# Weight-quarter sums of a hybrid layer's feed-forwards: from vector additions to accumulating DMAs in DRAM, with seven and five tiles done by quarters instead of six and four

## The chip, the cores and the metric

The kernel runs on one core of one Trainium2 chip. The metric is device time in microseconds (us) of one execution; the median over several runs is compared. The core has TensorE (PE, the matrix unit, with PEld for its weight loads), VectorE (DVE), ScalarE (ACT) and GpSimd (POOL), which compute, and SyncE (SP), which in this kernel does nothing but issue DMAs. Each engine works through its own queue of instructions in order and waits on semaphores for the others. A DMA is issued by an engine's queue and then runs beside the engines. SBUF is the on-chip memory with 128 partitions, PSUM holds the results of TensorE (eight banks of 128x512 fp32), and DRAM is the memory outside.

## The reference

One layer, batch 1, 512 tokens (T), width 1024 (D), fp32:

```python
x = x + 0.5 * rms_norm(swiglu_ffn(rms_norm(x, g0), ffn1_w_in, ffn1_w_out), p0)
x = x +       rms_norm(token_mixer(rms_norm(x, g1), ...), p1)
x = x + 0.5 * rms_norm(swiglu_ffn(rms_norm(x, g2), ffn2_w_in, ffn2_w_out), p2)

def swiglu_ffn(x, w_in, w_out):            # w_in 1024 x 5632, w_out 2816 x 1024
    gate, up = jnp.split(x @ w_in, 2, axis=-1)
    return (jax.nn.silu(gate) * up) @ w_out
```

`token_mixer` projects to 3592 columns, runs two causal mixers (HGRN2 with four heads, mLSTM with four heads) over the tokens, and projects back through a 1024 x 1024 matrix. The change touches only the second product of each feed-forward, `h @ w_out` with `h` 512 x 2816, and the places from which some of its preparation is issued.

## The kernel before

**Precision.** Every fp32 operand is split into a high part (rounded to fp32r by a cast) and a low part (the rest), and a product is three matmuls: high by high, high by low, low by high. A weight tile is 256 x 512 or 1024 x 128, 512 KB, 128 partitions by 1024 values. It is loaded by SP (`load`, L236) into a buffer of one of two rings, `raw` (three buffers) or `raw2` (five). ACT casts it into one of four weight slots (L273, the high part), and DVE subtracts to get the low part (L275). `split` holds these steps. `feed` calls it until four slots are taken, `pull` gives the next prepared tile to TensorE, `drop` frees its slot.

**Order.** The program is one Python generator run from top to bottom. `weights` walks a list of `Item`s, one for each tile that TensorE uses; an `Item` has a key and the `Load`s that belong to it. From the ring's depth and the `ahead` of a `Load`, `weights` works out after which item a load may be issued, and `load_due` issues it at the end of that item's `split`. `behind(...)` makes what is issued inside it follow the given instructions in the order of the scheduler, which otherwise places instructions of each engine by their dependencies. Most SP waits are for a ring's buffer to be read by ACT and DVE.

**Feed-forward, first product.** `ffn_in` runs through `ORDER` (or `ORDER2` in the second feed-forward), a list of pairs (product, tile). There are eleven tiles of 256 hidden rows. Each is made with seven products instead of eight, of halves of the inner dimension, of the columns and of the tokens (`prod`, matmuls at L603, 24 for each product). Sums of weights that these need are made by DVE in the raw buffers (L289). At the end all hidden values lie in `hf`.

**Feed-forward, second product.** `ffn_out` makes two halves of 512 output columns, one after the other. For each half it goes through the eleven tiles in the order `OUT[half]`. For every (half, tile) a weight tile of 256 hidden rows by 512 columns is used. It is done in one of two ways.

- *Plainly* (`plain`, L893): four blocks of 128 tokens, two of 256 columns, two of 128 hidden rows, three matmuls: 48 matmuls of 256 columns each.
- *By quarters* (`quartered` and `product`, L901), for the tiles in `QUARTERED[half]`. The weight tile is four quarters of 128 hidden rows by 256 columns, and the hidden tile is four quarters as well. Seven products of six matmuls, 42 in all, take sums of quarters on both sides (the Strassen-Winograd scheme). Four of the products go to banks shared by all such tiles of the half (`M`), three straight into the output's banks `C`. After the half's last tile by quarters `common` (L925) combines the four shared banks into `T`, and `add` (L863 in the half's last matmuls) adds these into the output.

Such a tile pulls two weight tiles: first the quarters as loaded, less quarter 0 which no product needs (so the split has 768 columns), then their four sums. `sum_quarters` (L306) makes these on DVE, four additions of 128x256 in place in the raw buffer, as the last thing that the first split does; the second `Item` has no load and reads the same buffer.

On the hidden side `h_quarters` splits the left quarters (ACT L812, DVE L813), either into places in buffers that held the input (`PLACES`, tiles 2, 4, 6, 8) or into two buffers of the ring `raw`. `h_sums` makes the sums of the hidden quarters (DVE L844, four additions), `s_tile` splits these. `more(n)` keeps such work two to three tiles ahead of TensorE. What is made for a tile stays for the second half if that half also does it by quarters. A plain tile's hidden part is `h_tile`; `LATER` gives buffers to some of them, and those in `AGAIN` are kept from the first half.

The last four tiles of the second half (`LAST`) are done otherwise: all four weight tiles are held, one in each slot, and TensorE goes through them token block by token block, so that the norm behind the product (`last`, `post1`) can begin with the first tokens.

**Mixers.** Between the feed-forwards `mixer` runs the projection's products as jobs: `job_f` (columns as partitions, for forget gates, queries and convolution inputs), `job_t` (tokens as partitions: `hi`, `mv`, `hg`, `mo`). Each `pull`s weight tiles as it goes. Between the jobs' matmuls stand the recurrences, where POOL makes masks: selector masks (L1201) in the HGRN2 part, and the causal mask of the mLSTM scores (L1480), which stands between ACT's exponent (L1479) and DVE's product with the scores (L1490). Before the change POOL's queue issues no DMA there.

## Time and profile before

| | us |
|---|---|
| median of three runs | 936.34 |
| lowest, highest | 936.26, 937.92 |
| the profiled execution, its own time | 936.35 |
| the span of that execution in the profile | 934.6 |

The page of the profile gives the span from the first to the last instruction of the profiled execution, so that about 1.75 us of that execution's time lie outside. The stages in the trace, by the rows in which their instructions run: the first feed-forward's first product up to 224 us, its second product from there to 341.8, the mixers and their output projection to about 560, the second feed-forward's first product to 810.8, and its second product with the norm and the stores to the end.

In the rows of the groups, a line gives the source line, the engine, the operation, the tile written and the tile read with partitions x elements, the count, the busy time and the mean of one in ns, and behind the last bar the idle time of the engine just before these instructions with what ended it. In the rows of a stretch of time the columns are: from and to, length, then busy time and count of PE, PEld, DVE, ACT and POOL, the granted clock of TensorE, the busy share of the DMA engines, and GB/s. In the rows of the timeline they are: start, length, engine, line, operation, tile written and tile read, form, and how many like instructions were joined; idle time before it stands in brackets. A DMA's row in the issues gives the tile, the queue, the count, the size and the median time from issue to landing.

### The profile page before, as it was taken

Reading aid. Unit: us, or ns where it says so; the run is one execution under the profiler, and the core shown is the slowest. Engines: PE = TensorE matmul, PEld = TensorE weight load, DVE = VectorE, ACT = ScalarE, POOL = GpSimd, SP = SyncE. Lnnn points to the kernel's source line nnn. Section 1 sums busy time; section 2 is a strip of 40 time slices with the busy share of each in tenths; the row PEclk is TensorE's granted clock in tenths of the full one; section 3 lists DMA queues with packets and bytes.
Section 4 is the critical chain, followed back from the end, with each engine's and each line's share of the span. In section 5 each row is a group of like instructions: output and inputs, shape, how many; then the busy total and the mean of one; then the engine's idle time right before and its main releaser. Section 6 shows DMA issues by size and latency. Waiting matters only on the chain.

```text
span 934.6 us, 18052 instructions
## 1 busy us (share of the span) xinstructions
PE 926.2 (99%) x7471; PEld 891.8 (95%) x7471; DVE 772.1 (83%) x1044; ACT 511.4 (55%) x735; POOL 106.5 (11%) x172
## 2 busy tenths in 40 slices
PE   9999999999999999999999999999999999999997
PEld 7999999999999999998887887899999999999997
DVE  6899988889988877698766565799899889998884
ACT  7645454557456466956533445595454545655541
POOL 3530000000001045200010310313000000000101
PEclk9999999999999999999999999999999999999999
DMA  9253343332352025421212124352354435334212
GB/s 313 94 157 91 119 132 113 93 112 71 114 177 91 24 72 134 114 70 54 81 46 69 46 91 150 98 181 70 112 158 136 136 116 159 111 91 126 79 46 91
DMA packets 86956, 101.35 MB, mean 108 GB/s; under 512 B 4277, under 2 KB 66777, under 8 KB 86874
## 3 DMA queue, kind: packets, MB, share of 16 engines
q1 hardware_dynamic: 86586, 99.68, 34.9%
q8 instruction: 58, 0.95, 0.4%
q10 hardware_dynamic: 288, 0.52, 0.2%
q14 instruction: 24, 0.20, 0.1%
HBM read 98.10 MB, written 2.10 MB: 107 GB/s over the span
## 4 chain that ended last, share of the span: by engine, by line
PE 62%; ACT 1%; issue 0%; DVE 0%; POOL 0%; DVEq 0%; POOLq 0%; ACTq 0%
PE ps L603 22%; PE ps L893 7%; PE ps L533 6%; PE ps L901 5%; PE ps L179 5%; PE ps L181 5%; PE ps L180 5%; PE ps L1307 2%; PE ps L348 1%; PE ps L543 1%; PE ps L1488 0%; PE ps L1399 0%; PE ps L1600 0%; PE ps L1573 0%; PE ps L1353 0%; PE ps L1597 0%
## 5 line engine op out<-in xcount | busy, mean ns | idle before, releaser
L273 ACT CAST w<-raw 128x1024 fp32r<-128x1024 f32 (+1 forms) x238 | 244.4, 1035 | 231.7 <-PE ps L603 92.8
L275 DVE TENSOR_TENSOR w<-raw,w 128x1024 fp32r<-128x1024 f32 (+1 forms) x238 | 290.9, 1229 | 38.0 <-ACT w L273 37.5
L603 PE MATMUL ps<-xq,w 128*128 128x256 f32 x2016 | 237.1, 277 | 0.0
L603 PEld LDWEIGHTS ps<-xq,w 128*128 128x128 f32 x2016 | 232.9, 188 | 0.0
L603 PE MATMUL ps<-sq,w 128*128 128x256 f32 x1512 | 178.0, 276 | 0.3
L603 PEld LDWEIGHTS ps<-sq,w 128*128 128x128 f32 x1512 | 174.3, 188 | 1.1 <-ACT ps L654 0.9
L893 PE MATMUL ps<-w,hs 128*128 128x256 f32 x960 | 113.0, 276 | 0.0
L893 PEld LDWEIGHTS ps<-w,hs 128*128 128x128 f32 x960 | 110.7, 188 | 0.0
L289 DVE TENSOR_TENSOR raw<-raw,raw 128x1024 f32<-128x1024 f32 x72 | 89.8, 1251 | 8.3 <-DMA raw<-in_ffn_w_in_dram 6.7
L179 PE MATMUL ps<-w,xq 128*128 128x512 f32 x192 | 78.0, 407 | 0.1
L180 PE MATMUL ps<-w,xq 128*128 128x512 f32 x192 | 74.9, 391 | 0.0
L181 PE MATMUL ps<-w,xq 128*128 128x512 f32 x192 | 74.9, 392 | 0.0
L438 POOL TENSOR_SCALAR col<-col 128x1 f32<-128x1 f32 x24 | 8.3, 347 | 513.4 <-ACT junk L437 513.3
L901 PE MATMUL ps<-w,hs 128*128 128x256 f32 x480 | 57.7, 276 | 0.0
L901 PEld LDWEIGHTS ps<-w,hs 128*128 128x128 f32 x480 | 55.9, 188 | 0.0
L533 PE MATMUL ps<-xq,w 128*128 128x256 f32 x480 | 55.7, 278 | 0.0
L533 PEld LDWEIGHTS ps<-xq,w 128*128 128x128 f32 x480 | 54.9, 188 | 0.5 <-issue 0.5
L179 PEld LDWEIGHTS ps<-w,xq 128*128 128x128 f32 x192 | 36.1, 188 | 8.5 <-issue 0.9
L181 PEld LDWEIGHTS ps<-w,xq 128*128 128x128 f32 x192 | 36.0, 188 | 8.0 <-DVE xq L355 0.3
L812 ACT CAST hs<-hf 128x1024 fp32r<-128x1024 f32 x32 | 33.7, 1052 | 17.5 <-PE ps L901 10.8
L180 PEld LDWEIGHTS ps<-w,xq 128*128 128x128 f32 x192 | 36.1, 188 | 7.3 <-DVE w L281 0.3
L813 DVE TENSOR_TENSOR hs<-hf,hs 128x1024 fp32r<-128x1024 f32 x32 | 39.0, 1217 | 1.3 <-ACT hs L812 1.2
(259 smaller groups left out, 1136.8 us busy)
## 6 DMA issues: line engine op xcount, KB each, us to landing
raw<-in_ffn_w_in_dram SPq DMA_DIRECT2D x98, 512.0 KB, 3.7
raw<-in_ffn_w_out_dram SPq DMA_DIRECT2D x44, 512.0 KB, 4.3
raw<-in_w_mix_in_dram SPq DMA_DIRECT2D x28, 512.0 KB, 3.7
raw<-in_w_mix_out_dram SPq DMA_DIRECT2D x8, 512.0 KB, 3.9
out_dram<-xs SPq DMA_DIRECT2D x8, 256.0 KB, 2.0
xs<-in_x_dram SPq DMA_DIRECT2D x6, 256.0 KB, 4.5
gpost<-in_norm_post_dram SPq DMA_DIRECT2D x3, 512.0 KB, 3.6
gpre<-in_norm_pre_dram SPq DMA_DIRECT2D x2, 512.0 KB, 4.8
```

The lines of the kernel that those rows point to most:

```text
L179: mm(ps, sh, mh, start=start, stop=False, **kw)
L180: mm(ps, sh, ml, start=False, stop=False, **kw)
L181: mm(ps, sl, mh, start=False, stop=stop, **kw)
L273: nc.scalar.copy(hi, raw)
L275: self.low = nc.vector.tensor_tensor(lo, raw, hi.bitcast(F32), op=ALU.subtract)
L289: (nc.vector if late else nc.gpsimd).tensor_tensor(o, o, c, op=ALU.add)
L533: mm(ps[:, u0:u1], w[:, a, k, :], self.xop(k, b, u0, u1), start=k + n + m == 0, stop=k == ND - 1 and n == 2, skip_group_check=True,)
L603: self.nc.tensor.matmul(ps[:, c], wb[b][:, k, v], left[d][:, k, :], start=first and a + n + k == 0, stop=n == 2 and k == KH - 1, skip_grou ...
L812: self.nc.scalar.copy(hi, src)
L813: self.nc.vector.tensor_tensor(lo, src, hi.bitcast(F32), op=ALU.subtract)
L893: mm(out, a[kk][:, i * P : (i + 1) * P], w[:, b, kk, QUARTER * v : QUARTER * (v + 1)], start=begin and c == kk == n == 0, stop=kk == 1 and ...
L901: mm(ps[:, QUARTER * c : QUARTER * (c + 1)], A[a][:, c], B[b], start=begin and c == n == 0, stop=n == 2, skip_group_check=True,)
```

## The change

Four things change together.

1. The sums of weight quarters are no longer made by DVE in the raw buffer. A tile in DRAM is kept for each (feed-forward, half, tile by quarters), 24 of them, each four quarters of 128x256. `sums_ahead` fills one. Three copies on SP's queue bring quarter 1, quarter 2 and quarters 2 and 3 of the weights from DRAM to DRAM. Then three DMAs on POOL's queue add: first quarter 0 to the first two, then the first of these to the quarter behind it, then that quarter to the last. Each needs the one before it. The result is in the order (0, 1, 2, 3) of a list that `quartered` reads with `at = (1, 0, 2, 3)`.
2. The second `Item` of a tile by quarters now has a `Load` of its own, of the 512 KB of sums from DRAM into ring `raw2`, where it had none.
3. `sums_due` says for which feed-forward and halves sums are to be made, and each call of `make_sums` starts one tile and moves those under way one step further. The first feed-forward's are made during its `ffn_in`, every fifth product after the fourteenth, and at every other tile of the first half of its `ffn_out`. The second's first half is made in the mixers, at each job of the convolution and each weight tile of `hi` and `mv`; its second half in its own `ffn_in`, every tenth product, and in the first half of its `ffn_out`.
4. Seven tiles are done by quarters in the first half (5 is new) and five in the second (3 is new), in each feed-forward. The order of the second half changes. The left quarters of tiles 5 and 7, which have no place of their own, take one buffer of ring `raw` and the buffer `gpre`, where they took two of `raw`. Tile 0's hidden part loses its place among `LATER`. The last two additions of `h_sums` become one of twice the width.

The diff:

```diff
@@ -79,12 +79,13 @@
-QUARTERED = [(2, 3, 4, 6, 7, 8), (2, 4, 6, 8)]
-OUT = [list(range(PAIRS)), [9, 2, 4, 10, 6, 8, 0, 1, 3, 5, 7]]
-LAST = 4
-PLACES, LATER = {2: 1, 4: 2, 6: 0, 8: 3}, {0: (1, 0), 7: (2, 3)}
+QUARTERED = [(2, 3, 4, 5, 6, 7, 8), (2, 3, 4, 6, 8)]
+OUT = [list(range(PAIRS)), [9, 2, 4, 3, 6, 8, 10, 0, 1, 7, 5]]
+LAST, APART = 4, (5, 7)
+PLACES, LATER = {2: 1, 4: 2, 6: 0, 8: 3}, {7: (2, 3)}
 AGAIN, ROWS = (9, 10), (18, 19, 20, 21)
+EVERY = 5, 10
@@ -136,6 +137,11 @@
         x0 = self.xt[0].rearrange("p (b x) -> p b x", b=2)[:, :, :D].rearrange("p b (k t) -> p b k t", k=KH)
         self.xh = [x0, *self.xq[1:]]
         self.prm = self.cp.tile([P, 36], F32, name="prm")
+        dram = ctx.enter_context(tc.tile_pool(name="sums", bufs=1, space=bass.MemoryType.DRAM))
+        self.sums_of = {
+            (f, h, k2): dram.tile([P, 4, QUARTER], F32, name=f"{f}sums{h}_{k2}")
+            for f in ("f1", "f2") for h in range(2) for k2 in OUT[h] if k2 in QUARTERED[h]
+        }
     def nm(self, s):
         self.uid += 1
@@ -287,8 +293,6 @@
                 late = out[1] >= (HEAD if out[0] == "f1" else 1)
                 (nc.vector if late else nc.gpsimd).tensor_tensor(o, o, c, op=ALU.add)
-        if it.sums:
-            self.sum_quarters(self.quarters(self.raw[it.key]))
         self.load_due(self.done)
         self.done += 1
         yield
@@ -299,11 +303,6 @@
     def quarters(self, v):
         v = self.flat(v)
         return [v[:, QUARTER * j : QUARTER * (j + 1)] for j in range(4)]
-
-    def sum_quarters(self, b):
-
-        for out, a, c in ((1, 1, 0), (0, 0, 2), (2, 1, 2), (3, 2, 3)):
-            self.nc.vector.tensor_tensor(b[out], b[a], b[c], op=ALU.add)
     def both(self, w):
@@ -782,7 +781,10 @@
     def ffn_in(self):
-        for p, t in ORDER2[len(HEADS2) :] if self.second else ORDER[len(HEADS) :]:
+        self.sums_due("f2" if self.second else "f1", (1,) if self.second else (0, 1))
+        for n, (p, t) in enumerate(ORDER2[len(HEADS2) :] if self.second else ORDER[len(HEADS) :]):
+            if n > 14 and n % EVERY[self.second] == 0:
+                self.make_sums()
             with self.behind(*(self.c22 if p == "p3" and self.second else ())):
                 self.feed()
             self.c22 = []
@@ -822,9 +824,12 @@
     def h_quarters(self, k2, n=None):
         src = self.by_chunk(k2)
-        parts = self.x_place(n) if n is not None else [
-            self.wp.tile([P, D], F32R, tag="raw", bufs=RAW, name=self.nm("once"))[:, P - 2 * STEP :] for _ in range(2)
-        ]
+        once = lambda pool, tag, bufs, o: pool.tile([P, D], F32R, tag=tag, bufs=bufs, name=self.nm("once"))[:, o:]
+        if n is not None:
+            parts = self.x_place(n)
+        else:
+            places = [(self.wp, "raw", RAW, P - 2 * STEP), (self.cp, "gpre", 1, STEP // 2)]
+            parts = [once(*places[k2 in APART and m]) for m in range(2)]
         parts = [v[:, : 3 * QUARTER].rearrange("p (k c t) -> p k c t", c=2, t=P) for v in parts]
         self.two_parts(*(v[:, 0] for v in parts), src[:, 0, 1])
         self.two_parts(*(v[:, 1:] for v in parts), src[:, 1])
@@ -844,8 +849,7 @@
         tt = lambda out, x, y, op: self.nc.vector.tensor_tensor(out, x, y, op=op)
         tt(v[:, 0, 0], a[:, 0, 1], a[:, 0, 0], ALU.subtract)
         tt(v[:, 1, 0], v[:, 0, 0], a[:, 1, 0], ALU.add)
-        for k in range(2):
-            tt(v[:, k, 1], a[:, k, 1], v[:, 1, 0], ALU.subtract)
+        tt(v[:, :, 1], a[:, :, 1], v[:, 1:2, 0].broadcast_to([P, 2, 2, P]), ALU.subtract)
         return f
     def s_tile(self, f):
@@ -854,6 +858,29 @@
         self.two_parts(*parts, f)
         parts = [t.rearrange("p k (c u t) -> p k u c t", u=2, t=P) for t in parts]
         return [[t[:, j // 2, j % 2] for j in range(4)] for t in parts]
+
+    def sums_ahead(self, f, h, k2):
+
+        nc, to = self.nc, self.sums_of[f, h, k2]
+        w = (self.ffn1_w_out, self.ffn2_w_out)[f == "f2"][0]
+        q = w[k2 * 2 * P : (k2 + 1) * 2 * P, h * 512 : (h + 1) * 512].rearrange("(k p) (c f) -> p k c f", p=P, f=QUARTER)
+        with self.behind(self.loaded):
+            nc.sync.dma_start(to[:, 0], q[:, 0, 1])
+            nc.sync.dma_start(to[:, 1], q[:, 1, 0])
+            nc.sync.dma_start(to[:, 2:], q[:, 1])
+        yield
+        for a, b, v in ((0, 2, q[:, 0, :1].broadcast_to([P, 2, QUARTER])), (2, 3, to[:, :1]), (3, 4, to[:, 2:3])):
+            nc.gpsimd.dma_start(to[:, a:b], v, accum_op=ALU.add)
+            yield
+
+    def sums_due(self, f, halves):
+        self.ahead, self.making = deque(k for k in self.sums_of if k[0] == f and k[1] in halves), []
+
+    def make_sums(self):
+
+        if self.ahead:
+            self.making.append(self.sums_ahead(*self.ahead.popleft()))
+        self.making = [g for g in self.making if next(g, self) is not self]
     def ffn_out(self, gpost_row, scale, after, trans, head):
@@ -912,11 +939,11 @@
             product(C[1][1], A(3), quarter(w, 3), False)
             product(C[1][0], S(3), quarter(w, 2), False)
             self.drop(w)
-            v = self.pull()
-            product(M["p7"], S(0), quarter(v, 0), begin)
-            product(M["p5"], S(1), quarter(v, 1), begin)
-            product(M["p6"], S(2), quarter(v, 2), begin)
-            product(C[0][1], A(2), quarter(v, 3), False)
+            v, at = self.pull(), (1, 0, 2, 3)
+            product(M["p7"], S(0), quarter(v, at[0]), begin)
+            product(M["p5"], S(1), quarter(v, at[1]), begin)
+            product(M["p6"], S(2), quarter(v, at[2]), begin)
+            product(C[0][1], A(2), quarter(v, at[3]), False)
             self.drop(v)
         def common(M, t):
@@ -965,6 +992,8 @@
                             add(C, T, i % 2)
                     self.drop(w)
                 n += 1
+                if half == 0 and n % 2:
+                    self.make_sums()
                 if n == 1:
                     self.prod("p4", PAIRS - 1)
                     self.after("p4", PAIRS - 1)
@@ -1017,6 +1046,8 @@
     def job_f(self, name, then):
         w, ps = self.pull(), self.ps()
+        if name[0] == "c":
+            self.make_sums()
         for k in range(ND):
             self.in_k(ps, w, k, [(0, HALF), (HALF, T)])
             if k < ND - 1:
@@ -1035,6 +1066,8 @@
         acc = [self.ps() for _ in range(NT)]
         for k2 in range(ND // 2):
             w = self.pull()
+            if name in ("hi", "mv"):
+                self.make_sums()
             for i in range(NT):
                 for kk in range(2):
                     self.t_mm(acc[i], w, 2 * k2 + kk, kk, i)
@@ -1124,9 +1157,11 @@
             for k2 in OUT[h]:
                 src = w_out[k2 * 2 * P : (k2 + 1) * 2 * P, h * 512 : (h + 1) * 512].rearrange("(k p) d -> p k d", p=P)
                 key = (name, "out", h, k2)
-                made.append(Item(key, [Load(key, src, 2, 512, "raw2", 5, 8)], sums=k2 in QUARTERED[h]))
-                if k2 in QUARTERED[h]:
-                    made.append(Item(key, ()))
+                four = k2 in QUARTERED[h]
+                made.append(Item(key, [Load(key, src, 2, 512, "raw2", 5, 8)], sums=four))
+                if four:
+                    key, src = (*key, "sums"), self.sums_of[name, h, k2].rearrange("p (a j) f -> p a (j f)", a=2)
+                    made.append(Item(key, [Load(key, src, 2, 512, "raw2", 5, 8)]))
                 if h == k2 == 0:
                     made.append(Item((name, PAIRS - 1, "a"), ()))
         return made
@@ -1636,6 +1671,7 @@
     def mixer(self):
         nc, tc = self.nc, self.tc
         self.got, self.jobs = set(), deque()
+        self.sums_due("f2", (0,))
         with tc.tile_pool(name="ma", bufs=1) as ma:
             self.vh = ma.tile([P, NT, NH, P], F32, name="vh")
             self.vm = ma.tile([P, NT, NH, 129], F32, name="vm")
```

## The prediction

> **What bounds the kernel now.** I read the page first: busy time, slices, the chain that ended last.
>
> ```profile
> span 934.6 us, 18052 instructions
> PE 926.2 (99%) x7471; PEld 891.8 (95%) x7471; DVE 772.1 (83%) x1044; ACT 511.4 (55%) x735; POOL 106.5 (11%) x172
> PE   9999999999999999999999999999999999999997
> PEclk9999999999999999999999999999999999999999
> PE 62%; ACT 1%; issue 0%; DVE 0%; POOL 0%; DVEq 0%; POOLq 0%; ACTq 0%
> ```
>
> TensorE is busy in 99% of the span and in every slice but the last, at the full granted clock, and no other engine has a visible share of the chain. A busy PE row alone doesn't say that its matmuls follow at their pace, so the next view is the busy time by stretch: start and end, length, then PE, weight loads, DVE, ACT, POOL, clock, DMA share and GB/s.
>
> ```profile
> 56.00:112.00 56.00, 56.00 (x495) 56.00 (x494) 55.59 (x65) 27.80 (x33) 1.30 (x1) 1.00 0.47 142
> 224.00:341.76 117.76, 117.68 (x1038) 117.48 (x1037) 101.28 (x153) 62.87 (x101) 10.17 (x27) 1.00 0.28 86
> 810.80:934.60 123.80, 117.78 (x1040) 117.59 (x1038) 99.89 (x149) 57.93 (x88) 7.05 (x20) 0.99 0.28 90
> ```
>
> The second and third are the two output projections, the only stages where the arithmetic changes. PE has no gap there except after the last matmul; DVE is busy for 101.28 of 117.76 us. The price of one matmul comes from the timeline of PE (start, length, row, count):
>
> ```profile
> 239.00 2.88 PE L901 MATMUL ps<-w,hs 128*128 128x256 f32 x24
> 241.72 0.84 PE L901 MATMUL ps<-w,xq 128*128 128x256 f32 x6
> 312.44 5.60 PE L893 MATMUL ps<-w,xq 128*128 128x256 f32 x48
> 317.88 4.24 PE L893 MATMUL ps<-w,hs 128*128 128x256 f32 x36
> ```
>
> 24 quarter products take 241.72 - 239.00 = 2.72 us, 48 plain ones 317.88 - 312.44 = 5.44 us: 0.1133 us each, either way. (The mean of one in the groups is latency; the matmuls overlap.) A tile done plainly is 48 matmuls, 5.44 us; by quarters 7 products of 6, 42 matmuls, 4.76 us.
>
> **The change, part by part.** *Tiles.* Each feed-forward goes from six and four tiles by quarters to seven and five, so 2 x 2 x 6 = 24 matmuls go: 24 x 0.1133 = 2.72 us. They lie on PE, which sets the end. No PE instruction is added.
>
> *The quarter sums leave DVE, and the four new tiles cost splits.* Rows of the groups (count, busy, mean ns), then single ones:
>
> ```profile
> L306 DVE TENSOR_TENSOR raw<-raw 128x256 f32<-128x256 f32 x80 | 33.7, 421 | 1.6
> L844 DVE TENSOR_TENSOR hf<-hf 128x256 f32<-128x256 f32 x32 | 13.3, 419 | 0.5
> L813 DVE TENSOR_TENSOR hs<-hf,hs 128x1024 fp32r<-128x1024 f32 x32 | 39.0, 1217 | 1.3 <-ACT hs L812 1.2
> L813 DVE TENSOR_TENSOR once<-hf,once 128x256 fp32r<-128x256 f32 (+1 forms) x8 | 4.4, 549 | 0.0
> L812 ACT CAST once<-hf 128x256 fp32r<-128x256 f32 (+1 forms) x8 | 3.8, 511 | 1.8 <-DVE w L275 1.8
> L812 ACT CAST hs<-hf 128x1024 fp32r<-128x1024 f32 x32 | 33.7, 1052 | 17.5 <-PE ps L901 10.8 <-DVE hf L844 4.4 <-PE ps L893 2.3
> 225.24 0.95 DVE L275 TENSOR_TENSOR w<-raw,w 128x768 fp32r<-128x768 f32 x1
> 223.61 0.84 ACT L273 CAST w<-raw 128x768 fp32r<-128x768 f32 x1
> ```
>
> DVE loses 80 sums, 33.7 us. It gains four splits of 768 columns (4 x 0.95), four pieces of left quarters for tile 5 (4 x 0.55), and the sums of hidden tiles, four instructions for each of 12, become three for each of 14, the third twice as wide; priced as two it makes 14 x 4 x 0.42 - 12 x 4 x 0.42 = 3.4. Net 33.7 - 3.8 - 2.2 - 3.4 = 24 us less. ACT gains 4 x 0.84 + 4 x 0.51 = 5.4 us. Neither moves the end: DVE and ACT are hidden by PE in both stages already, so I take 0 for what they gain as well. Through the run of seven quarter tiles DVE needs, per tile, splits of 0.95 and 1.2, 1.22 for the sums of the hidden tile and at most 2.8 for tiles met first: 6.2 us against 4.76 of PE. Before it was 1.7 more (4 x 0.421) and PE had no gap, because much of this is done ahead, in the input projection; the cover grows.
>
> *Two places get tighter.* Tiles 5 and 7 share one buffer for their left quarters, so 7's are made only when PE has finished 5. PE then has tile 6, 4.76 us; the work is the sums of tile 8 on ACT and DVE (1.05 + 1.22) and two pieces of left quarters on DVE (2 x 0.55), 3.4 us. It fits by 1.4. The second is the end of the second half, seen before as:
>
> ```profile
> 318.08 1.05 ACT L273 CAST w<-raw 128x1024 fp32r<-128x1024 f32 x1 [4.06 <-PE ps L893]
> 318.33 1.28 DVE L863 TENSOR_TENSOR ps<-ps,hf 128x512 f32<-128x512 f32 x2
> 319.52 1.21 DVE L275 TENSOR_TENSOR w<-raw,w 128x1024 fp32r<-128x1024 f32 x1
> 321.96 1.52 PE L893 MATMUL ps<-w,xq 128*128 128x256 f32 x12
> ```
>
> The last weight tile is split by 320.73 and used at 321.96: 1.23 us to spare. Now tile 10 holds a buffer until then, so tile 5's hidden part is made in the same place, one more 1.05 on ACT and 1.22 on DVE ahead of that split. Nothing is left to spare; a few tenths are lost, or up to 1.2 us if ACT is late too, in each feed-forward. I take 0.1 each, 0.2 together (0 and 2.4 as ends).
>
> *The DMAs.* Per tile three copies on SP's queue (128, 128, 256 KB, DRAM to DRAM), three accumulations on POOL's queue (256, 128, 128 KB), and a 512 KB load of the sums; 24 tiles: 72 + 72 + 24. No row shows a DRAM-to-DRAM or an accumulating transfer, so bounds (us to landing; then what SP waited for):
>
> ```profile
> q1 hardware_dynamic: 86586, 99.68, 34.9%
> raw<-in_ffn_w_out_dram SPq DMA_DIRECT2D x44, 512.0 KB, 4.3
> gpre<-in_norm_pre_dram SPq DMA_DIRECT2D x2, 512.0 KB, 4.8
> out_dram<-xs SPq DMA_DIRECT2D x8, 256.0 KB, 2.0
> SPq L236 <- DVE w L275: 630.2, 130, 36.8
> ```
>
> A landing takes 2.0 to 4.8 us for plain ones; an accumulation reads its target besides, so twice the upper end, 9.6, is my top. I take 4. Bytes: 99.7 MB took 34.9%; 3 x 12.6 MB more give about 48%, and twice for accumulations 53%: no stretch fills. SP waited 630 us for buffers, so its 96 more issues find room. Loads: two per quarter tile in a ring of five, so 2.5 tiles or 11.9 us ahead, against 4.3 to land. A load of sums now waits on SP for its third accumulation, and the next weight loads stand behind it; in the first half of each feed-forward that accumulation was issued long before. Two loads of mixer weights and the next norm's gain wait on SP for PE to release left quarters (tile 7, then tile 3): at most the rest of a tile, 4.76 us, inside the 11.9. All of this I cost at 0, hidden by PE; if that cover is gone, the split behind a late load is late, and PE after four weight tiles.
>
> *POOL's queue.* An accumulation waits there for the one before it on the same tile, and everything behind it waits too. Behind the sums of the feed-forwards' second halves stand only statistics of the first half, on which the next step of POOL works 37 us later (the last row below, idle time in brackets). In the mixers it matters: seven tiles' sums stand between the selector masks and the causal masks of the mLSTM heads.
>
> ```profile
> 379.68 3.29 POOL L1201 CAST selr<-sel 4x768 fp32r<-4x768 f32 x2
> 391.57 0.37 SPq L236 DMA_DIRECT2D raw<-in_w_mix_in_dram  x1
> 427.81 0.39 PE L179 MATMUL ps<-w,xq 128*128 128x512 f32 x1
> 428.03 0.39 PE L180 MATMUL ps<-w,xq 128*128 128x512 f32 x1
> 441.51 0.37 SPq L236 DMA_DIRECT2D raw<-in_w_mix_in_dram  x1
> 480.45 1.39 POOL L1513 MEMSET C<- 128x1548 f32 x1 [97.48 <-DVE sT L1312]
> 488.14 0.83 POOL L1480 TENSOR_SCALAR_AFFINE_SELECT e<-e 128x512 f32<-128x512 f32 x1 [6.30 <-ACT e L1479]
> 488.38 1.67 DVE L275 TENSOR_TENSOR w<-raw,w 128x1024 fp32r<-128x1024 f32 x1
> 489.97 0.68 DVE L1490 SCALAR_TENSOR_TENSOR pT<-ps,e 128x512 f32<-128x512 f32 x1
> 912.99 0.27 POOL L438 TENSOR_SCALAR col<-col,col 128x1 f32<-128x1 f32 x1 [36.80 <-ACT junk L437]
> ```
>
> The first copies follow the load at 391.57, the last that at 441.51; the first causal mask runs at 488.14 and DVE needs it at 489.97. POOL is empty between 383 and 480. In the order of its queue two tiles are interleaved twice, so the seven wait for 12 landings and 9 issues (0.37 each, as SP's): with 4 us that is 51 us of work, paced by the copies: the last land by 446.3 and are done by 455, 33 us early. Cost 0. DVE's 1.67 instead of 1.21 beside a POOL instruction shows that the two can hold each other up; 0.46 x 72 = 33 us, spread where DVE has just been given 24, moves nothing on PE.
>
> For an accumulation's landing only a page has a price: the Trainium skill, DMA: Bandwidth & Descriptors, section "Anatomy of one DMA — SWDGE (gpsimd) path", gives 2.0 us plus bytes over 436 GB/s; an estimate from it is 2.6 us for 256 KB, and the sum would be the same. A rule speaks against the change: the Trainium skill, SBUF — State Buffer, section "SBUF: two separate sides", says that a DMA issued from POOL can't get its descriptors written while DVE runs an operation that takes the port pair which both share. An estimate by the page's example (3.1 instead of 0.62 us) makes each landing 2.5 us longer, 5.1 us: still nothing on PE, but most of the way to the first rival. No run here shows it yet.
>
> *Sum.* The profiled execution took 936.35 us, span 934.6, and the median is 936.34: 936.35 - 2.72 + 0.2 = 933.8.
>
> **The rivals.** *POOL's queue takes over (slower).* From 396.4 (first copies landed) to 488.14 are 91.7 us; 12 landings and 3.3 us of issues fit up to 7.4 us each. At 9.6 they end at 515, 27 us late; DVE stands at the row of 489.97, weight splits behind it, and PE runs on four weight tiles of 24 x 0.22 = 5.3 us at most. Some 6 to 27 us are lost, I take 12: 946. For it: nothing shows such a transfer. Against: 7.4 is above every landing seen. Chance 0.18.
>
> *The gain is eaten (no change).* The end of the second half loses 1.2 us in each feed-forward, or sums land late once: 936.35 - 2.72 + 2.4 = 936.0. For it: no slack is left there. Against: DVE arrives at both stages with less behind it. Chance 0.18.
>
> *Another gain (it is not only the matmuls).* DVE was the hidden pace and its relief shortens the stages: 1038 matmuls in 117.68 us are 0.1134 each, so at most a few tenths a stage, 932.8 in all. Chance 0.04.
>
> **How the numbers follow.** My forecast, 933.8, has 0.60, between 933.3 and 934.4. What a measurement can tell from no change is about 0.2%, 1.9 us: under 934.5 counts as faster, over 938.2 as slower. The forecast and the third rival are faster, less 0.02 of the forecast that lies over the line; the second rival and most of that are the same; the first is slower, with 0.01 for what I don't see: 0.62, 0.19, 0.19. The range leaves out most of the first rival and reaches over the second: 932.8 to 938.5.
>
> **What would show it.** After: 24 matmuls fewer, pitch still 0.1133, the output stages 1.4 us shorter each; L306 gone and DVE some 24 us lower; POOL's causal mask within a microsecond of ACT's exponent; PE without a wait for a sums load. Wrong would be: landings over 7 us, DVE waiting at the score product for POOL, or PE waiting in the last four tiles of the second half.

## The result, and the profile after

The changed kernel takes 938.1 us in the median of 22 runs (935.98 to 940.84), the kernel before 936.94 us beside it: a ratio of 1.0015, 95% interval 1.0009 to 1.0021. By that ratio it is slower by 1.4 us, less than the 0.2% that the prediction called no change; 933.8 us and a gain of 2.7 us were forecast. A second set of 11 runs (`change_again`) gave 937.76 against 937.0, 1.0011 (0.9999 to 1.0022).

The page of the profile after: span, busy time, two of the queues, and landings (count, KB, median us).

```profile
span 936.2 us, 18261 instructions
PE 924.4 (99%) x7447; PEld 889.9 (95%) x7447; DVE 751.0 (80%) x966; ACT 516.7 (55%) x743; POOL 174.8 (19%) x244
q1 hardware_dynamic: 100410, 124.85, 43.0%
q0 software_dynamic: 13440, 12.59, 10.2%
raw<-in_ffn_w_in_dram SPq DMA_DIRECT2D x98, 512.0 KB, 4.8
f1sums<-in_ffn_w_out_dram POOLq DMA_DIRECT2D x12, 256.0 KB, 7.6
f2sums<-in_ffn_w_out_dram SPq DMA_DIRECT2D x24, 128.0 KB, 3.8
f2sums<-in_ffn_w_out_dram SPq DMA_DIRECT2D x12, 256.0 KB, 6.7
f2sums<-in_ffn_w_out_dram POOLq DMA_DIRECT2D x12, 256.0 KB, 6.9
f2sums<-f2sums POOLq DMA_DIRECT2D x24, 128.0 KB, 3.5
```

24 matmuls are gone, and DVE has 21 us less. But PE, which waited nowhere in the second feed-forward's input projection, now waits there once. L621 (L622 before) holds DVE's operations on finished products in PSUM; here it is a subtraction for which PE's next product waits. First that wait of PE after, then DVE's timeline up to it, after and (last fence) before:

```profile
PE ps L602 <- DVE ps L621: 2.1, 1, 2.1
```

```profile
761.37 1.22 DVE L295 TENSOR_TENSOR raw<-raw,raw 128x1024 f32<-128x1024 f32 x1 [4.27 <-DMA raw<-in_ffn_w_in_dram]
762.52 0.69 DVE L621 TENSOR_TENSOR ps<-ps,hf 128x512 f32<-128x512 f32 x1
...
772.38 0.69 DVE L621 TENSOR_TENSOR ps<-ps,hf 128x512 f32<-128x512 f32 x1
773.22 1.05 PE L602 MATMUL ps<-sq,w 128*128 128x256 f32 x7 [2.15 <-DVE ps L621]
```

```profile
759.65 1.23 DVE L289 TENSOR_TENSOR raw<-raw,raw 128x1024 f32<-128x1024 f32 x1 [2.54 <-DMA raw<-in_ffn_w_in_dram]
760.79 0.69 DVE L622 TENSOR_TENSOR ps<-ps,hf 128x512 f32<-128x512 f32 x1
...
770.66 0.69 DVE L622 TENSOR_TENSOR ps<-ps,hf 128x512 f32<-128x512 f32 x1
```

A weight load lands 1.72 us later (761.37 against 759.65). From there DVE works without a pause to the subtraction that PE needs, in both kernels, so all of it arrives at PE; PE itself is 0.37 us ahead there, and so it waits 2.1. The load in question was issued at the same time in both kernels, after and then before:

```profile
754.26 0.37 SPq L242 DMA_DIRECT2D raw<-in_ffn_w_in_dram  x1
```

```profile
754.27 0.94 SPq L236 DMA_DIRECT2D raw<-in_ffn_w_in_dram  x1
```

These two traces have no landing for it. `copies_at_the_place` and `sums_alone`, below, have: there the load issued at this place lands at 761.22 and 761.25, and DVE's addition starts 0.12 later. So the load takes longer. What changed is the traffic. From 752 to 762 us, after and then before (DMA share and GB/s at the end):

```profile
752.00:762.00 10.00, 9.91 (x87) 9.71 (x87) 5.73 (x6) 3.04 (x4) 1.17 (x1) 1.00 0.95 249
```

```profile
752.00:762.00 10.00, 9.91 (x88) 9.71 (x87) 7.46 (x8) 3.89 (x6) 0.00 (x0) 1.00 0.62 197
```

The copies for the third tile of the second half were issued at 749.95 to 751.14, the first accumulation at 754.64.

The end is late too. The program's closing line, after and then before (ns min/median/max, first and last start):

```profile
L1861 POOLq DRAIN  x3: 38/102/5013, 930.4 to 935.9; - x3
L1861 SPq DRAIN  x3: 7/7/7, 934.5 to 935.6; - x3
```

```profile
L1825 POOLq DRAIN  x3: 39/78/656, 929.7 to 934.4; - x3
L1825 SPq DRAIN  x3: 7/7/7, 933.9 to 934.2; - x3
```

POOL's closing drain takes 5.01 instead of 0.66 us. It starts at 930.36 behind POOL's last instruction and ends at 935.37, 0.8 us after SP is done with the stores. Before, it was over 3.5 us ahead of SP.

The start of each matmul after, less its start before, tells where the time went (us, along the time of before; worked out from both traces, for this kernel and those of the experiments):

| | 36 | 220 | 338 | 670 | 768 | 790 | last matmul |
|---|---|---|---|---|---|---|---|
| the change | 0.09 | 0.09 | -1.27 | -1.18 | -0.37 | 1.73 | 0.37 |
| change_again | 0.25 | 0.25 | -1.11 | -0.99 | -1.01 | 1.05 | -0.31 |
| tiles_alone | 1.18 | 1.18 | 1.94 | 1.97 | 2.03 | 2.43 | 2.97 |
| copies_alone | 0.67 | 0.66 | -0.70 | -0.68 | -0.65 | 1.04 | -0.32 |
| copies_at_the_place | 0.70 | 0.70 | 0.70 | 0.79 | 0.79 | 1.71 | 1.71 |
| sums_earlier | 0.58 | 0.58 | -0.78 | -0.65 | 8.82 | 8.52 | 7.16 |
| second_in_first | 0.50 | 0.50 | 8.04 | 8.30 | 8.52 | 8.70 | 7.34 |
| first_alone | -0.15 | -0.15 | -1.51 | -1.52 | -1.52 | -0.92 | -0.92 |
| all_but_last_again | 0.79 | 0.79 | -0.57 | -0.43 | -0.24 | 0.27 | -0.11 |

Each output projection gives its 1.36 us, twice (0.09 to -1.27, and 1.73 to 0.37). The sum of the profile: -2.72, start 0.09, drift 0.09, slower pace of the matmuls from 677 to 697 us 0.81, the wait 2.10, ACT's last statistic 0.28 later behind PE, drain and closing 0.87: 1.52, and the spans differ by 1.53. The first column is chance: before, profiled again, is itself 0.72 late there. So is part of the pace: the change's second profile has no slower stretch at 677, but the wait of 2.1 and the drain again.

### The profile page after: what moved, and what is told of

It is laid out like the page before. It is cut to its first block, busy times and chain, and to the rows that moved or that the text cites. A ratio compares the mean times of both kernels' runs of the same rounds, so it can differ in the third digit from the quotient of the medians.

```text
span 936.2 us, 18261 instructions
## 1 busy us (share of the span) xinstructions
PE 924.4 (99%) x7447; PEld 889.9 (95%) x7447; DVE 751.0 (80%) x966; ACT 516.7 (55%) x743; POOL 174.8 (19%) x244
## 4 chain that ended last, share of the span: by engine, by line
PE 62%; ACT 1%; DVE 0%; issue 0%; POOL 0%; DVEq 0%; POOLq 0%; ACTq 0%
PE ps L602 22%; PE ps L928 6%; PE ps L532 6%; PE ps L920 6%; PE ps L185 5%; PE ps L187 5%; PE ps L186 5%; PE ps L1342 2%; PE ps L347 1%; PE ps L542 1%; PE ps L1523 0%; PE ps L1434 0%; PE ps L1635 0%; PE ps L1608 0%; PE ps L1388 0%; PE ps L1632 0%
## 5 line engine op out<-in xcount | busy, mean ns | idle before, releaser
L279 ACT CAST w<-raw 128x1024 fp32r<-128x1024 f32 (+1 forms) x242 | 248.1, 1031 | 206.3 <-PE ps L602 91.2
L281 DVE TENSOR_TENSOR w<-raw,w 128x1024 fp32r<-128x1024 f32 (+1 forms) x242 | 295.7, 1225 | 36.7 <-ACT w L279 35.6
L814 ACT CAST hs<-hf 128x1024 fp32r<-128x1024 f32 x34 | 35.8, 1053 | 37.0 <-PE ps L928 22.0
L815 DVE TENSOR_TENSOR hs<-hf,hs 128x1024 fp32r<-128x1024 f32 x34 | 41.5, 1222 | 18.2 <-ACT hs L814 18.1
L873 POOL DMA_DIRECT2D f2sums<-in_ffn_w_out_dram x12 | 15.9, 1322 | 133.2 <-DMA f2sums<-in_ffn_w_out_dram 133.0
```

Source lines behind the costliest of these rows:

```text
L279: nc.scalar.copy(hi, raw)
L281: self.low = nc.vector.tensor_tensor(lo, raw, hi.bitcast(F32), op=ALU.subtract)
L814: self.nc.scalar.copy(hi, src)
L815: self.nc.vector.tensor_tensor(lo, src, hi.bitcast(F32), op=ALU.subtract)
```

## The experiments

**The two parts apart.** The tiles, the order and the places of the change, with `sum_quarters` kept on DVE and no DMAs:

```diff
-QUARTERED = [(2, 3, 4, 6, 7, 8), (2, 4, 6, 8)]
+QUARTERED = [(2, 3, 4, 5, 6, 7, 8), (2, 3, 4, 6, 8)]
...
```

> Seven and five tiles by quarters, in the new order and with the new places, but the sums of weight quarters made by DVE in the raw buffers as before: no DMA in DRAM, none on POOL's queue. Theory A (the tiles give the 2.72 us that the matmuls are worth, and the DMAs take it back by late weight loads and by POOL's closing drain): 936.9 - 2.7 = 934.2 us, PE 2.7 us less busy and no wait on PE over 0.5 us. Theory B (DVE, or the new order, eats the gain): 936 to 938 us, with a wait of PE on a split or on a hidden tile in an output projection.

940.2 us, 1.0032 (1.0020 to 1.0043). Theory B, and more than it foresaw: with the sums still on DVE the tiles cost time. Instead of gaining 1.36 us the two output projections lose 0.76 and 0.54 (table). PE's waits there that are long enough to be listed (in all, times, longest), then the busy times in the run of seven tiles, here and (last fence) in the change:

```profile
PE ps L903 <- DVE w L275: 1.9, 4, 0.7
```

```profile
249.00:274.00 25.00, 24.12 (x207) 23.72 (x206) 24.48 (x35) 16.12 (x19) 0.00 (x0) 1.00 0.36 115
```

```profile
249.00:274.00 25.00, 25.00 (x223) 25.00 (x223) 19.89 (x22) 15.60 (x18) 2.84 (x3) 1.00 0.94 276
```

DVE is full, 24.48 of 25 us, and PE has 16 matmuls fewer in it. In the change DVE has 5 us to spare there. So the gain is had only if sums leave DVE in the run of seven tiles. Those of the second half matter less: `first_halves`, below, leaves them on DVE and loses 0.3 us for it.

The other part alone, the sums in DRAM with the old tiles and order:

```diff
-QUARTERED = [(2, 3, 4, 5, 6, 7, 8), (2, 3, 4, 6, 8)]
+QUARTERED = [(2, 3, 4, 6, 7, 8), (2, 4, 6, 8)]
...
```

> Six and four tiles by quarters in the old order, but the sums made in DRAM by the DMAs (60 accumulations instead of 72). Theory A: 936.9 + 2.1 (PE waiting for DVE's L621 in the second feed-forward's input projection) + 0.9 (POOL's closing drain, 5.0 instead of 0.7 us) = 939.9 us. Theory B: 936.9 us.

938.88 us, 1.0020 (1.0011 to 1.0028). PE waits 0.9 us for L621 at the same place, less than half of what was expected; the drain takes 4.03 us and is hidden. The median is 2.1 us up; 0.9 of it is this wait, and the rest is not explained.

**Where the second half's sums are made.** In the mixers (`sums_due("f2", (0, 1))`, from the query jobs on):

> The change, but the sums of the second feed-forward's second half are made in the mixers as well (from the query jobs on), so that no copy and no accumulation is issued during its input projection. Theory A: the wait of 2.1 us on DVE's L621 is gone, 938.1 - 2.1 = 936.0 us, closing drain still 5 us. Theory B (the late DVE there is chance or comes from elsewhere): 938.1 us. If POOL's queue were too full in the mixers: over 940 us, with DVE waiting at the score product for the causal mask.

950.76 us, 1.0138. The wait for L621 is gone, and the prediction's first rival is there. POOL's queue, then DVE's and PE's waits:

```profile
504.29 0.81 POOL L874 DMA_DIRECT2D f2sums<-f2sums  x1 [2.50 <-DMA f2sums<-f2sums]
506.48 1.24 POOL L1516 TENSOR_SCALAR_AFFINE_SELECT e<-e 128x512 f32<-128x512 f32 x2
```

```profile
DVE pT L1526 <- POOL e L1516: 17.6, 1, 17.6
```

```profile
PE ps L1524 <- DVE pT L1526: 12.4, 1, 12.4
```

Twelve tiles keep the queue until 505 us, and the causal masks, wanted at 488, wait. In the change itself seven tiles are issued by 471.8, with 15 us to spare:

```profile
471.00 0.81 POOL L873 DMA_DIRECT2D f2sums<-f2sums  x1 [2.85 <-DMA f2sums<-f2sums]
...
486.89 0.83 POOL L1515 TENSOR_SCALAR_AFFINE_SELECT e<-e 128x512 f32<-128x512 f32 x1 [6.30 <-ACT e L1514]
```

Every fifth product of the input projection instead of every tenth:

```diff
-EVERY = 5, 10
+EVERY = 5, 5
```

> The change, with the sums of the second feed-forward's second half begun every fifth product of its input projection instead of every tenth (at 15, 20, 25, 30, 35 instead of 20, 30, 40, 50, 60), so that all copies and accumulations are over before the place at 750 to 773 us. Theory A (transfers beside the weight loads make a load late at a place where DVE has nothing to spare): PE's wait for L621 at 773 us falls from 2.1 to under 0.5, 938.1 - 2 = 936 us. Theory B (DVE is late there by chance, whatever the transfers): 938 us.

945.71 us, 1.0091. The wait at 773 went, as the theory says, and three others came, at the same subtraction, at 710, 745 and 764 us. It is not one bad place: denser traffic meets more of them.

```profile
PE ps L602 <- DVE ps L621: 4.7, 3, 2.1
```

The table shows 9.5 us lost from 670 to 768, twice these waits. The next largest part is the granted clock (the 1.00 behind POOL in the other rows): it falls behind the waits at 710 and 764 us, of 2.1 and 1.8 us, which costs 1.7 us each time, 0.42 of 4 us and 0.19 of 9 us:

```profile
711.00:715.00 4.00, 4.00 (x24) 4.00 (x22) 3.02 (x6) 1.89 (x3) 1.00 (x1) 0.58 0.90 256
760.00:769.00 9.00, 7.22 (x49) 7.04 (x47) 6.87 (x8) 1.05 (x2) 0.00 (x0) 0.81 0.66 211
```

In the profile of the change, behind a wait as long, the clock stays at 1.00.

In the first feed-forward, behind its own (`sums_due(("f1", 0), ("f1", 1), ("f2", 1))`, `EVERY = 4`, the list no longer reset):

> The change, but the sums of the second feed-forward's second half are made in the first feed-forward, behind its own (one tile begun every fourth product of its input projection, the rest in its output projection); the mixers keep those of the first half, and the second feed-forward's input projection issues no copy and no accumulation. All 72 accumulations stay. Theory A: no wait for L621 over 0.6 us, so 938.1 - 1.5 to 2.1 = 936.0 to 936.6 us, with a closing drain of 5 us. Theory B (the second feed-forward is late whatever is issued there): 938 us. If the first feed-forward's input projection has as little to spare as the second's: waits of PE on DVE there instead, 938 us or more.

947.32 us, 1.0107. No wait for L621 in the second feed-forward, but 7.0 us in the first one's output projection. POOL, ACT, DVE and PE's wait:

```profile
295.61 0.81 POOL L875 DMA_DIRECT2D f2sums<-f2sums  x1 [2.59 <-DMA f2sums<-f2sums]
```

```profile
296.69 0.38 ACT L437 ACTIVATE junk<-ps 128x256 f32<-128x256 f32 x1 [11.43 <-POOL col L438]
```

```profile
297.19 0.98 DVE L475 TENSOR_TENSOR y<-ps,gpost 128x256 f32<-128x256 f32 x2 [11.48 <-ACT junk L437]
```

```profile
PE ps L930 <- DVE y L475: 7.0, 1, 7.0
```

The statistics of the first half stand in POOL's queue behind the last accumulations. ACT gets no new column until POOL has used the old ones, DVE waits for ACT, and PE for the banks that DVE has still to read. Here too the clock falls, to 0.59 from 297 to 302 us, and in `second_in_mixers` to 0.52 from 507 to 514.

**What makes the load late.** The change with the second half's 15 accumulations left out in the second feed-forward, the copies kept:

> The change, but the 15 accumulations of the second feed-forward's second half are left out (its output is then not the layer's); the copies and the loads of the sums stay. If the copies alone delay the weight load: PE's wait for L621 at 773 us stays 1.5 to 2.1, 937.5 to 938 us. If the accumulations do: under 0.5, 936.0 us. The closing drain, with 57 accumulations, about 3.8 us and hidden: 0.8 us less in both.

936.08 us, 0.9988 (0.9979 to 0.9996). The wait is still 1.7 us: it needs no accumulation of these. The closing drain takes 3.79 us, and nothing waits for it.

Then the same three copies put into the kernel before, first at product 50, which turned out to be the wrong place, then at 40:

```diff
+            if self.second and n == 40:
...
+                with self.behind(self.loaded):
+                    self.nc.sync.dma_start(self.to[:, 0], q[:, 0, 1])
+                    self.nc.sync.dma_start(self.to[:, 1], q[:, 1, 0])
+                    self.nc.sync.dma_start(self.to[:, 2:], q[:, 1])
```

> The kernel before, with nothing added but three copies in DRAM (512 KB in all, of one weight tile, into a tile that nobody reads) on SP's queue at the fiftieth product of the second feed-forward's input projection, where the change issues those of its fourth tile. Theory A (bytes of copies beside the weight loads make the load late by their own transfer): PE waits 1.5 to 2.1 us for L621 near 772 us, 936.9 + 1.5 = 938.4 us. Theory B (the accumulations, or the earlier tiles and the new order, make it): no more than the 0.3 to 0.6 us seen there without transfers, 937 us.

936.8 us, 1.0001 (0.9993 to 1.0010), no wait: issued at 780 us, as the change's own fourth tile, they cost nothing that the trace shows.

> As copies_into_before (three copies in DRAM added to the kernel before, no accumulation), but ten products earlier, so that they are issued near 750 us, where the change issues those of its third tile, instead of near 780. Theory A (copies beside the group of weight loads of 753 to 757 us make the last one late): PE waits 1.5 to 2.1 us for L621 near 772 us, 938.5 us. Theory B: under 0.6 us there, 937.0 us.

939.44 us, 1.0026 (1.0015 to 1.0037); issued at 751.4 us, PE waits:

```profile
PE ps L605 <- DVE ps L624: 1.0, 1, 1.0
```

512 KB of copies, at that place, are enough to make a kernel that waits nowhere wait 1.0 us. (The median is up by 2.3 us; what the rest is, the one trace doesn't show.)

That the change waits twice as long has a second part, which the traces separate. Of the load in question: how much later it is issued, measured against PE's own place in the program, and the time from its issue to DVE's addition (us); then what PE loses at the subtraction.

| | issued later | issue to addition | PE loses |
|---|---|---|---|
| before | 0 | 5.38 | 0 |
| copies_at_the_place | 0.03 | 6.26 | 0.92 |
| sums_alone | -0.22 | 6.44 | 0.93 |
| tiles_alone | 0.65 | 5.04 | 0.40 |
| all_but_last_again (below) | 0.64 | 5.25 | 0.51 |
| copies_alone | 0.62 | 6.44 | 1.69 |
| change_again | 0.60 | 6.31 | 2.07 |
| the change | 0.37 | 7.11 | 2.11 |

Beside copies the load takes 6.3 to 7.1 us, and 4.9 to 5.6 in the kernels without copies there. Accumulations add nothing in `sums_alone` and `change_again`; the 0.7 more in the first profile of the change stays open. The later issue comes with the fifth tile, not with the traffic, as `tiles_alone` and `all_but_last_again` have it without copies: the tile's hidden sums (`h_sums`) are made ahead, here, on the DVE that must free the buffers for the loads. Two loads, 3.0 us apart in the trace of before, are 3.6 apart with them (750.14 and 753.14; 749.53 and 753.13). The longest of these sums in the change:

```profile
749.43 0.68 DVE L849 TENSOR_TENSOR hsum<-hf,hsum 128x512 f32<-128x512 f32 x1
```

Not every kernel feels it: in `first_halves` and `second_in_first` the loads around this place run earlier against PE, and no wait over 0.2 us comes of it.

**The change without that traffic.** First the change in the first feed-forward alone:

> The change in the first feed-forward alone: seven and five tiles and sums in DRAM there; six and four tiles with DVE's sums in the second, no DMA on POOL's queue behind the first. Theory A (all the loss lies in the second feed-forward's input projection and in the closing drain): 936.8 - 1.36 = 935.4 us, closing drain about 2.4 us and hidden. Theory B: 936.8 us or more.

935.99 us, 0.9990 (0.9981 to 0.9998). No wait of PE over 0.2 us past the start; the 0.6 us between 768 and 790 in the table are a slower pace. The first feed-forward's share of the gain, 1.36 us, is whole.

Then in both, with only the first halves' sums in DRAM and DVE adding those of the second halves:

> Seven and five tiles as in the change, but only the sums of the first halves are made in DRAM (14 tiles, 42 accumulations: the first feed-forward's in its input projection, the second's in the mixers); the sums of the second halves are made by DVE in the raw buffers. Theory A (the gain of 2.72 us is whole where neither the second feed-forward's input projection sees a transfer nor DVE makes sums in the run of seven tiles, which is where tiles_alone lost it): no wait of PE over 0.6 us, closing drain about 3.6 us and hidden, 937.0 - 2.7 + 0.3 = 934.6 us. Theory C (DVE's sums in the second half cost as much there as in the first): 936.5 us with waits of PE on a split in the second halves.

936.37 us, 0.9989 (0.9980 to 0.9998). No wait for L621; 0.3 us lost in each second half; in its profile 445 matmuls of the mixers and just ahead ran at the slower pace.

Last the whole change but for the last five sums, which DVE makes:

```diff
-            for f in ("f1", "f2") for h in range(2) for k2 in OUT[h] if k2 in QUARTERED[h]
+            for f in ("f1", "f2") for h in range(2) for k2 in OUT[h] if k2 in QUARTERED[h] and (f, h) != ("f2", 1)
...
+        if it.sums and it.key[0] == "f2" and it.key[2] == 1:
+            b = self.quarters(self.raw[it.key])
+            for out, a, c in ((1, 1, 0), (0, 0, 2), (2, 1, 2), (3, 2, 3)):
+                nc.vector.tensor_tensor(b[out], b[a], b[c], op=ALU.add)
...
```

> The change, except that the five sums of the second feed-forward's second half are made by DVE in the raw buffers, so that its input projection issues no copy and no accumulation; the first feed-forward's twelve and the second's first seven stay in DRAM (57 accumulations). Theory A: no wait of PE for L621, 0.3 us lost to DVE's sums in that one half (first_halves lost 0.3 in each), closing drain about 3.8 us and hidden: 937.0 - 2.7 + 0.3 = 934.6 us, or up to 1 us more by the slower pace of matmuls that some executions show. Theory B (the gain does not come back): 937 us.

936.32 us, 0.9992 (0.9983 to 1.0001).

> all_but_last a second time. Its first profile was 2.3 us ahead of before at 898 us when the later start is taken off, its median only 0.6. If that is start and pace alone, the median is again 935 to 936.3 us and the stages in the trace again give 2.3 us, with no wait of PE over 0.3 us; if a wait comes and goes from execution to execution, it should show here.

935.64 us, 0.9981 (0.9972 to 0.9990). Up to 898 us its traces are 2.3 us (first) and 1.9 us (second, with a wait of 0.6 us for the subtraction near 772) ahead of before once the later start is taken off; in each 1.0 is lost again, 0.3 at 910 us, where PE's loading of weights (PEld) waits for DVE's split of the last tile, and 0.7 by a slower pace from there to 928. The second set is clearly faster than before, the first not quite; in both the median lies under that of the change.

**The drain and chance.**

> The kernel before, with one of its two loads of gate biases (16 bytes) issued from POOL's queue instead of SP's. If POOL's closing drain has a fixed price once a DMA has been issued from its queue: drain 5.0 us, the end 0.9 us later, 937.8 us. If the drain's price goes by the number of such DMAs: 0.7 us, 936.9 us.

938.06 us, 1.0016 (1.0008 to 1.0025), with a drain of 0.745 us: a single DMA doesn't bring its full price.

> one_pool_dma a second time. Its median was 1.3 us above before, its profile showed the 1.3 us in the first 12 us and a closing drain of 0.74. If one DMA on POOL's queue costs this at the start each time: 938.1 us and a start 1.3 us late again; if it was chance: 936.9 us.

937.86 us, 1.0011 (1.0002 to 1.0020), starting 0.9 us late. A second time the median is higher, by 0.5 us, but before itself can start 0.7 late; where that half microsecond lies was not found.

> The kernel before, unchanged, profiled a second time: 936.9 us. It tells what of the differences between profiles is chance: the start (the first matmuls of the input projection begin up to 1.5 us later in some profiles than in that of before) and the stretches of about 130 matmuls at a 4% slower pace (0.6 to 0.8 us each), which have been seen in seven of the twelve profiles with DMAs on POOL's queue and in none of the four without.

937.18 us, 1.0000 (0.9991 to 1.0009).

> The change as it is, profiled a second time. What belongs to it comes again: PE's wait for L621 near 773 us of 1.5 to 2.1, a closing drain of 5.0 us that ends 0.8 us behind SP, 938.1 us. What was chance in the first profile does not: the slower pace of the matmuls between 677 and 698 us (0.8 us).

Told above: the wait and the drain came again, the slow stretch did not.

> As sums_earlier, and a drain of POOL's queue is put behind the first half of the second feed-forward's output projection, behind all accumulations. If the closing drain works off what the accumulations left: the early one takes 4 to 5 us beside other work, the closing one 0.7, and the end is 0.8 us earlier than in sums_earlier. If it is the same work each time: closing drain 5 us again and the time of sums_earlier.

> As second_in_first, with a drain of POOL's queue placed behind the split of the last tile of the second feed-forward's first half, so behind all accumulations. If a drain works off what the accumulations left: this one takes 4 to 5 us beside other work, the closing one 0.7, and the time is 0.8 us less than second_in_first. If every drain costs the same: closing drain 5 us, same time as second_in_first.

943.85 and 949.57 us, as their bases (945.71 and 947.32) within the spread of 4 to 6 runs. Both times the added drain was placed at 5 to 6 us, ahead of every accumulation, and the closing one took 5.01 us. Whether an early drain would take over the closing one's work stays open.

## Why the prediction was wrong

- *Tiles, -2.72 us: right.* 1.36 us in each output projection, in the change, in `change_again` and in `copies_alone`, and in the first feed-forward of `first_alone`.
- *"The quarter sums leave DVE": right in size, wrong in "neither moves the end".* 21 us less were measured where 24 were reckoned. The prediction costed the tiles on PE and let DVE count for nothing either way; `tiles_alone` shows that without the relief the tiles lose. And the work that the new tile brings, its hidden sums, moves PE: the prediction had them "done ahead, in the input projection", where it did not price them. There they have a load issued some 0.6 us later, and PE in `all_but_last_again` loses 0.5 by it with no copies.
- *"Two places get tighter", 0.2 us: they cost nothing in the change.* Both output projections gain exactly 1.36 us. The second place does cost the "few tenths", 0.3, where DVE still makes the second half's sums (`first_halves`, `all_but_last`).
- *The DMAs, "all of this I cost at 0, hidden by PE": this step failed, and with it the cover that it names.* "53%: no stretch fills" was a mean over the span. The second feed-forward's input projection already moved its weights in bursts, with 0.62 in the ten microseconds that matter, and they filled to 0.95. The cover named was the depth of a ring in an output projection (11.9 us), but the delayed load belongs to the input projection, where a row of the trace of before already had DVE waiting 2.54 us for a load. The price there is 2.1 us. `copies_at_the_place` shows the cause, 1.0 us of it, by itself; the hidden sums make some 0.4 to 0.6 more.
- *POOL's queue: the place right, the price short, one cover wrong.* The prediction took 4 us a landing and 9.6 as the top; 6.9 and 3.5 were measured in the second feed-forward's (7.6 for the larger one in the first's, over the 7 that the prediction gave as a sign of being wrong), the seven tiles were through 20 us later than reckoned (471.8 plus 3.5, against 455) and still in time. The mechanism of the first rival decided in `second_in_mixers`, whose loss is 14.0 us by the medians. That this is near the rival's estimate of 12 is luck: the rival meant seven tiles, and here are twelve. Wrong was "only statistics of the first half, on which the next step of POOL works 37 us later": POOL's next use is far off, but ACT, DVE and PE are held at once, for 7.0 us in `second_in_first`.
- *The closing drain, 0.8 us: not foreseen.* No row of before shows what a queue with 72 DMAs leaves to be done.
- *The prices of the Trainium skill.* The Trainium skill, DMA: Bandwidth & Descriptors, section "Anatomy of one DMA — SWDGE (gpsimd) path", gave an estimate of 2.6 us for 256 KB; the trace has 6.9 and 7.6 for the accumulations, so it does not agree. They read their target as well and run beside other transfers; no run tells the two apart. The estimate of 5.1 us with the Trainium skill, SBUF — State Buffer, section "SBUF: two separate sides", is nearer but short too; no run here separates DVE's part in it. The Trainium skill, DMA: Bandwidth & Descriptors, section "SWDGE vs HWDGE vs iDMA", says that the queues of both kinds feed the same DMA engines, which serve them in turn. No run here shows that: the copies beside which the load was late are issued by SP, as the load is.

The wait and the drain together, 2.1 + 0.8, outweigh the 2.72 us of the matmuls; with 0.3 at ACT's last statistic they make 0.5 of the 0.8 to 1.4 us by which the medians are slower. The rest is not settled. The slower pace, 0.8 us in one of two profiles, is one part that the traces show. The clock may be another: five of the change's 33 executions, of 939.9 to 940.9 us, have a mean granted clock of 0.996 on record, where no execution of the kernel before that took 936 to 941 us has less than 0.998. `sums_earlier` shows such a fall behind a wait for the same subtraction; that it is the cause in these five was not profiled.

## What to carry to other kernels

A transfer that is hidden on the mean can still be on the path: look for the stage in which an engine already waits for a load by a little, take the DMA share of those ten microseconds and not of the span, and count what is added there, on the DMA engines and on the engine that frees the load's buffer. Work handed to an idle engine's queue holds up everything behind it, and who waits is found by following the queue's next instruction to its readers, not to the engine's next use. When two changes come together, run each alone: here one was worth nothing, or less, without the other.

## What the runs showed of the hardware that was not expected

- POOL's closing drain is longer in the kernels with DMAs on its queue, but not by their number alone: 0.66 us with none, 0.745 with 1, 3.62 with 36, 4.12 with 42 (`first_halves`), 3.79 with 57, 4.03 with 60, 5.01 with 72. In `first_alone` the last of them landed in the first feed-forward, some 650 us earlier, so it is not a wait for transfers.
- Waits of PE of the same length don't always bring the granted clock down: behind 2.1 us it fell in `sums_earlier` (0.58 from 711 to 715 us) and stayed at 1.00 in both profiles of the change.
- For stretches of about 130 matmuls the pace was 4% slower at a granted clock of 1.00. In these 20 us the change has 168 matmuls where the kernel before has 175:

```profile
677.00:697.00 20.00, 19.93 (x168) 19.72 (x168) 19.54 (x20) 10.06 (x14) 1.25 (x1) 1.00 0.77 200
```

```profile
678.00:698.00 20.00, 19.91 (x175) 19.71 (x174) 19.79 (x21) 10.77 (x15) 0.00 (x0) 1.00 0.58 185
```

Stretches of over 100 matmuls were seen only in kernels with DMAs on POOL's queue, in 8 of 15 such profiles and in none of the 5 without; `tiles_alone` has one of 75. The cause is open.
